# Moving half of the weight sums, and the second parts of weights, in a one-core decoder layer

## The chip, the cores and the metric

The kernel runs on one core of a Trainium2 chip. The core has five engines with instruction queues of their own: TensorE (PE; its weight loads are listed as PEld), VectorE (DVE), ScalarE (ACT), GpSimd (POOL) and SyncE (SP), which here issues nearly all DMAs. The metric is device time in microseconds (us) of one execution; the time before is the median of three runs. The profile is of one further execution.

## What is computed

One layer of a decoder, for a prompt of 2048 tokens and a sample group of 8 sequences of 8 tokens, with the same weights, in float32:

```python
def rmsnorm(x, w):
    return x * rsqrt(mean(x * x) + 1e-6) * w

proj = rmsnorm(x, norm_mix_w) @ w_in               # 1024 -> 8 x 512
rq, rk, rv, rg, hq, hf, hi, hg = split(proj, 8)    # 4 heads of 128 each
# retention heads: rotary on rq, rk; scalar decay per head
# HGRN2 heads: f = lb + (1 - lb) * sigmoid(hf), k = 1 - f
# both: S_t = diag(g_t) S_{t-1} + k_t^T v_t ;  o_t = q_t S_t   (chunkwise)
o = concat(head_rmsnorm(o_r) * silu(rg), head_rmsnorm(o_h) * silu(hg))
x = x + o @ w_out
x = x + square(relu(rmsnorm(x, norm_ffn_w) @ w_up)) @ w_down   # 1024 -> 4096 -> 1024
y = rmsnorm(x, final_norm_w)
```

The states S after the last token are outputs too.

## The kernel before, in words

The 2112 tokens are worked in three groups (`GROUPS`): 64 sample tokens with 512 of the prompt (576 columns), then twice 768 of the prompt. Each group goes through mixing (`mix`: per head the projections, then the recurrence in chunks of 128), the output projection, and the feed-forward. Activations stand with features on the 128 partitions and tokens along the row, in tiles of 768 columns ("slab", 46 of them, and 6 of a second kind, "ld").

Weights come as 128 x 1024 float32 blocks (512 KB). To multiply at nearly full float32 precision, each is split into two parts that TensorE's faster fp32r format can hold: `hi`, a rounded copy made by ScalarE (L269), and `lo` = raw - hi (L284), called the second part here, made by VectorE or GpSimd. Each product is hi x hi + hi x lo + lo x hi, three matmuls. `weight(i)` keeps two blocks ahead of the one in use; `hi` and `lo` have three buffers each, raw blocks of the first group two.

`plan_stream` lists the weights in order of use. For the first group, stream positions 0 to 39 are the input and output projections and 40 to 103 the 64 blocks of the feed-forward (`ffn_first`: up projections of one eighth of the 4096 features, `up_first`, then the down projections of the eighth before, `down_first`). The parts of positions 4 to 39 are written to DRAM once and read back ("p" entries) for groups two and three; only their first four blocks ("w" entries, positions 104 to 107 and 253 to 256) are split again.

Groups two and three compute their feed-forward with a seven-product scheme for 2 x 2 block products in place of eight (`PRODUCTS`, `OCTET`). It needs sums of weight blocks: S1 = A21 + A22, S3 = A11 - A21, S2 = S1 - A11, S4 = A12 - S2. `plan_sums` makes them: for each of 15 sets (7 of the up projection, 8 of the down projection), four loads, four VectorE additions of 128 x 1024 (L1273, tile `raw`), and four stores (L1278) to DRAM, from which the later groups load them as "s" entries.

The order of the work: the program puts instructions out in an order of its own and a scheduler orders them further within each engine; some are pinned with `keep_in_program_order` (the sums, their loads and stores among them). Each engine then works strictly in its order. In `proj`, every three-matmul product of a block calls `tick()`, which counts `n_ticks` and puts out whatever is due: work in `agenda` (through `at` and `later`) and the steps of `plan_sums` in `side`. So a tick is a place between matmuls, not a time. A block of weights has 8 sub-blocks with three products each: 24 ticks. The mixing of a later group has 4 heads with 192 ticks each, 768 in all; the first group's output projection and feed-forward have 192 + 1536 = 1728 ticks. Before, the 15 sets begin 90 ticks after the first mixing, one every 100 ticks, and within a set loads are at ticks 0, 12 and 24, additions at 40, 50, 60 and 70, stores at 60, 70, 80 and 90.

Other lines that matter: L1215 and L1151 are VectorE additions that empty a PSUM pair after a projection (`pj` has two pairs); L1202 and L1203 square the up projection's result on VectorE and cut it on GpSimd; L526 and L509 prepare the next group's input (`norm_in`); L1030 updates the state S, which L1017 multiplies (in a later group's head in 6 steps, one per chunk, 7 ticks apart); L348 and L482 cut tiles into two parts; L253 loads kept parts, L233 raw blocks.

The masks of the recurrence are 16 matrices of 128 x 128 zeros and ones, used as bytes (`msk`). `constants` gives them as float32; `masks` fetches them in four loads of 256 KB and GpSimd casts each to bytes (L451).

Of the kernel before, what the change touches and what calls it, by code (L numbers as in the profile page):

```python
# [15 lines left out]
P = 128  # L16
# [16 lines left out]
NLV = len(LEVELS) + 2  # L33
# [8 lines left out]
W_UP0 = W_OUT0 + N_OUT  # L42
W_DN0 = W_UP0 + N_UP
NQ = FF // (4 * P)
NO = NQ // 2

W_UQ0 = W_DN0 + N_DN
W_DQ0 = W_UQ0 + N_UP
# [50 lines left out]
def constants():  # L99
    c = np.zeros((P, NCONST), np.float64)  # L100
    c[:, C_ID:C_ID + P] = np.eye(P)
    s = np.arange(P)[:, None]
    t = np.arange(P)[None, :]
    sc = DK ** -0.5
    same = (s // SLEN == t // SLEN) & (s < NS) & (t < NS)
    for h, g in enumerate(GAM):
        dec = np.where(s <= t, g ** np.maximum(t - s, 0), 0.0) * sc
        c[:, C_RM + h * P:C_RM + (h + 1) * P] = dec
        c[:, C_RS + h * P:C_RS + (h + 1) * P] = np.where(same, dec, 0.0)
        c[:, C_GQ + h * P:C_GQ + (h + 1) * P] = g ** (t + 1.0)  # L110
        c[:, C_GS + h * NS:C_GS + (h + 1) * NS] = g ** (np.arange(NS) % SLEN + 1.0)
        c[:, C_KS + h] = sc * g ** (P - 1.0 - s[:, 0])
        c[:, C_KSS + h] = np.where(s[:, 0] < NS, sc * g ** (SLEN - 1.0 - s[:, 0] % SLEN), 0.0)
    c[:, C_SM:C_SM + NSEQ] = (s // SLEN == np.arange(NSEQ)[None, :])
    m = np.zeros((P, 2 * NLV, P), np.float32)
    for i, w in enumerate(LEVELS + (1,)):
        lv = (s // (2 * w) == t // (2 * w)) & (s % (2 * w) < w) & (t % (2 * w) >= w)
        m[:, i] = lv
        m[:, NLV + i] = lv & (s < NS) & (t < NS) & (w < SLEN)

    i = LEVELS.index(2)
    m[:, 0], m[:, NLV] = m[:, i] * (s % 2), m[:, NLV + i] * (s % 2)
    m[:, NLV - 1] = s == t
    m[:, 2 * NLV - 1] = (s == t) & (s < NS)
    half = DK // 2
    inv = np.power(10000.0, (-np.arange(half, dtype=np.float32) / np.float32(half)).astype(np.float64)).astype(np.float32)
    pos = np.concatenate([np.tile(PAST + np.arange(SLEN), NSEQ), np.arange(SEQ)]).astype(np.float32)
    ang = (inv[:, None] * pos[None, :]).astype(np.float64)
    cs = np.zeros((P, 2, NT), np.float32)
    cs[:half, 0] = cs[half:, 0] = np.cos(ang)  # L130
    cs[:half, 1] = -np.sin(ang)
    cs[half:, 1] = np.sin(ang)
    return c.astype(np.float32), m.reshape(P, -1), cs.reshape(P, -1)

# [63 lines left out]
class Kernel:  # L200
# [43 lines left out]
    def weight(self, i):  # L244
        n = len(self.stream)
        while self.w_next < min(i + 1 + self.ahead, n):
            j = self.w_next
            e = self.stream[j]
            if e[0] == "p":

                self.wts[j] = tuple(self.wp.tile([P, WT], F32R, tag=tag, name=tag) for tag in ("hi", "lo"))
                for part, kept in zip(self.wts[j], self.kept[e[1]]):
                    self.nc.sync.dma_start(part.bitcast(F32), kept)  # L253
                self.w_next += 1
                self.w_load = max(self.w_load, j + 1)
                continue
            while self.w_load <= j or j >= self.n_first and self.w_load <= j + 2 and self.w_load < n:
                if self.stream[self.w_load][0] == "p":
                    break
                k, later = self.w_load, self.w_load >= self.n_first  # L260
                raw = self.raws[k] = self.wp.tile([P, WT], F32, tag="sum" if later and k % 3 else "raw", name="raw",
                                                  bufs=4 if later and k % 3 else 2)
                e = self.stream[k]
                self.fetch(raw, self.sums[e[1]] if e[0] == "s" else self.I["w"][e[1]])
                self.w_load += 1
            raw = self.raws.pop(j)
            hi = self.wp.tile([P, WT], F32R, tag="hi", name="hi")
            lo = self.wp.tile([P, WT], F32R, tag="lo", name="lo")
            self.nc.scalar.copy(hi, raw)  # L269
            self.wts[j] = (hi, lo)  # L270
            self.second[j] = raw
            pool = self.stream[j][2] if len(self.stream[j]) > 2 else j % 4 and 3 < j
            if pool or j < 4:
                self.second_part(j, self.nc.gpsimd if pool else self.nc.vector)
            else:
                self.later(4, self.second_part, j, self.nc.vector)
            self.w_next += 1
        self.second_part(i, self.nc.vector)
        return self.wts[i]
# [87 lines left out]
    def build(self):  # L367
        nc, tc, I = self.nc, self.tc, self.I
        with ExitStack() as ctx:
# [19 lines left out]
            msk = cp.tile([P, 2 * NLV, P], U8, name="msk")  # L389
# [13 lines left out]
            for ns, p0, n in GROUPS:  # L403
# [4 lines left out]
                first = nch // 2  # L408
# [17 lines left out]
            nc.gpsimd.memset(self.ATs, 0.0)  # L426
            self.lower_bounds(cp)

            for i, g in enumerate(gs):
                nxt = gs[i + 1] if i + 1 < len(gs) else None  # L430
                if i == 0:
                    self.mix(g)
                    self.plan_sums(90, 100)
                    self.out_proj_first(g)
                    self.ffn_first(g, nxt)
                    continue
                if i == 1:
                    self.finish_first(gs[0])
                else:
                    self.finish(gs[i - 1])  # L440
                self.mix(g)
                self.out_proj(g)
                self.ffn(g, nxt)
            nc.sync.dma_start(self.O["ret_p"].rearrange("h d v -> d h v"), self.S[:, :H])
            nc.sync.dma_start(self.O["hg_p"].rearrange("h d v -> d h v"), self.S[:, H:])

    def masks(self):
        for i in range(0, 2 * NLV, 4):
            t = self.load()
            self.fetch(t[:, :4 * P], self.I["msk"][:, i * P:(i + 4) * P])  # L450
            self.nc.gpsimd.tensor_copy(self.msk[:, i:i + 4], t[:, :4 * P].rearrange("p (m t) -> p m t", t=P))  # L451

    def lower_bounds(self, cp):
        nc = self.nc
# [803 lines left out]
        self.later(4 * KB + 10, factor)  # L1258


    def plan_sums(self, first, every):
        nc, w = self.nc, self.I["w"]
        sets = [(("u", t), W_UQ0 + 4 * t) for t in range(1, NQ)]
        sets += [(("d", o, v), W_DQ0 + 4 * (2 * o + v)) for o in range(NO) for v in range(2)]
        self.side = deque()

        def load(x, i, *names):
            for name in names:
                x[name] = self.wp.tile([P, WT], F32, tag="sum", name="raw", bufs=4)
                self.tc.keep_in_program_order(nc.sync.dma_start(x[name], w[i + A_PLACE[name]]))  # L1270

        def make(x, name, a, op, b, into):
            self.tc.keep_in_program_order(nc.vector.tensor_tensor(out=x[into], in0=x[a], in1=x[b], op=op))  # L1273
            x[name] = x[into]

        def keep(x, key, name):
            s = self.sums[key + (name,)] = self.dp.tile([P, WT], F32, name="s" + "".join(map(str, key)) + name)
            self.tc.keep_in_program_order(nc.sync.dma_start(s, x[name]))  # L1278

        for j, (key, i) in enumerate(sets):  # L1280
            x, t = {}, self.n_ticks + first + every * j
            steps = [(0, load, x, i, "A21", "A22"), (12, load, x, i, "A11"), (24, load, x, i, "A12"),
                     (40, make, x, "S1", "A21", ALU.add, "A22", "A22"),
                     (50, make, x, "S3", "A11", ALU.subtract, "A21", "A21"),
                     (60, make, x, "S2", "S1", ALU.subtract, "A11", "A11"),
                     (70, make, x, "S4", "A12", ALU.subtract, "S2", "A12")]
            steps += [(d, keep, x, key, name) for d, name in ((60, "S1"), (70, "S3"), (80, "S2"), (90, "S4"))]
            for d, fn, *a in sorted(steps, key=lambda z: z[0]):
                self.side.append((t + d, lambda fn=fn, a=a: fn(*a)))
        self.side = deque(sorted(self.side, key=lambda z: z[0]))  # L1290
# [461 lines left out]
```

## Time and profile before

| | us |
|---|---|
| median of 3 runs | 2607.36 (2606.47 to 2609.86) |
| the profiled execution | 2605.96 |
| its span, first to last instruction | 2604.1 |
| TensorE busy | 2562.1 (98%) |
| VectorE busy | 1660.8 (64%) |
| ScalarE busy | 1161.2 (45%) |
| GpSimd busy | 932.4 (36%) |
| DMA | 441.32 MB, mean 169 GB/s |

How to read it: the times of the profile count from the first instruction. The first group's mixing ends near 300 us, its feed-forward near 796 us, the second group near 1690 us. Busy shares are means over stages with different limits, so the views of a stretch (windows, waits of one engine, timeline) say more than the page's totals. In the windows view each engine has its busy time and number of instructions, then the granted clock of TensorE, the share of the DMA engines' time, and GB/s. In a row of waits stand the engine and line that waited, the one that it waited for, total us, number, and longest. In a row of the timeline stand start, length, engine, line, operation, tiles, shape and count, and in brackets the idle time before it and what ended that. A group row has the count, busy time and mean duration in ns.

### The profile page before, as it was taken

Reading aid. Unit: us, or ns where it says so; the run is one execution under the profiler, and the core shown is the slowest. Engines: PE = TensorE matmul, PEld = TensorE weight load, DVE = VectorE, ACT = ScalarE, POOL = GpSimd, SP = SyncE. Lnnn points to the kernel's source line nnn. Section 1 sums busy time; section 2 is a strip of 40 time slices with the busy share of each in tenths; the row PEclk is TensorE's granted clock in tenths of the full one; section 3 lists DMA queues with packets and bytes.
Section 4 is the critical chain, followed back from the end, with each engine's and each line's share of the span. In section 5 each row is a group of like instructions: output and inputs, shape, how many; then the busy total and the mean of one; then the engine's idle time right before and its main releaser. Section 6 shows DMA issues by size and latency. Waiting matters only on the chain.

```text
span 2604.1 us, 41673 instructions
## 1 busy us (share of the span) xinstructions
PE 2562.1 (98%) x16999; PEld 2532.6 (97%) x16999; DVE 1660.8 (64%) x2072; ACT 1161.2 (45%) x1581; POOL 932.4 (36%) x538
## 2 busy tenths in 40 slices
PE   8999999999999999999999999999999999999997
PEld 8999999999999999999999999999999999999997
DVE  6666777554566455565554898775555555559876
ACT  6555442222244444444533544444444355345433
POOL 6555547444435133220222332341333012222322
PEclk9999999999999999999999999999999999999999
DMA  7566676666663322232555745442223326565542
GB/s 255 190 214 200 220 280 250 226 229 247 235 226 117 114 98 98 94 110 82 172 185 179 280 173 190 158 146 98 98 98 110 118 78 190 171 215 205 180 169 81
DMA packets 146689, 441.32 MB, mean 169 GB/s; under 512 B 14785, under 2 KB 36289, under 8 KB 146497
## 3 DMA queue, kind: packets, MB, share of 16 engines
q1 hardware_dynamic: 146352, 438.63, 49.1%
q8 instruction: 134, 2.20, 0.3%
q14 instruction: 59, 0.48, 0.1%
q10 hardware_dynamic: 144, 0.02, 0.0%
HBM read 330.85 MB, written 107.74 MB: 168 GB/s over the span
## 4 chain that ended last, share of the span: by engine, by line
PE 81%; DVE 4%; POOL 2%; issue 2%; ACT 1%; DMA 0%; DVEq 0%; POOLq 0%; ACTq 0%
PE pj L340 34%; PE pd L1123 16%; PE pu L1123 16%; PE pjv L705 5%; PE mm L1123 2%; PE mm L834 1%; PE po L1015 1%; PE mm L1023 1%; PE po L1017 1%; POOL lo L284 1%; DVE slab L509 1%; PE mm L891 1%; PE mm L488 1%; POOL slab L1178 1%; PE mm L487 1%
## 5 line engine op out<-in xcount | busy, mean ns | idle before, releaser
L340 PE MATMUL pj<-slab,hi 128*128 128x288 f32 (+1 forms) x5120 | 1016.2, 316 | 15.9 <-DVE slab L1215 7.2
L284 POOL TENSOR_TENSOR lo<-raw,hi 128x1024 fp32r<-128x1024 f32 x173 | 461.4, 2667 | 1079.4 <-ACT hi L269 993.8
L340 PEld LDWEIGHTS pj<-slab,hi 128*128 128x128 f32 x5120 | 810.9, 189 | 21.7 <-DVE slab L1215 8.1
L269 ACT CAST hi<-raw 128x1024 fp32r<-128x1024 f32 x330 | 347.0, 1051 | 746.9 <-PE pj L340 308.1
L340 PE MATMUL pj<-slab,lo 128*128 128x288 f32 (+1 forms) x2560 | 598.9, 315 | 1.4 <-POOL lo L284 1.2
L1123 PE MATMUL pd<-slab,hi 128*128 128x384 f32 x1792 | 456.9, 335 | 5.8 <-DVE slab L1568 2.1
L340 PEld LDWEIGHTS pj<-slab,lo 128*128 128x128 f32 x2560 | 429.2, 189 | 2.5 <-POOL lo L284 1.5
L1123 PE MATMUL pu<-slab,hi 128*128 128x384 f32 x1600 | 396.2, 334 | 0.0
L1123 PEld LDWEIGHTS pd<-slab,hi 128*128 128x128 f32 x1792 | 324.5, 188 | 7.1 <-DVE slab L1568 2.4
L284 DVE TENSOR_TENSOR lo<-raw,hi 128x1024 fp32r<-128x1024 f32 x157 | 208.3, 1327 | 146.2 <-ACT hi L269 142.9
L1123 PE MATMUL pd<-slab,lo 128*128 128x384 f32 x896 | 300.3, 335 | 0.9 <-POOL lo L284 0.9
L1123 PEld LDWEIGHTS pu<-slab,hi 128*128 128x128 f32 x1600 | 288.1, 188 | 0.0
L1123 PE MATMUL pu<-slab,lo 128*128 128x384 f32 x800 | 256.9, 334 | 0.0
L705 PE MATMUL pjv<-hi,slab 128*128 128x256 f32 x1088 | 208.5, 285 | 0.0
L1324 DVE TENSOR_TENSOR slab<-slab 128x768 fp32r<-128x768 f32 x144 | 162.0, 1140 | 33.4 <-ACT slab L1320 20.9
L705 PEld LDWEIGHTS pjv<-hi,slab 128*128 128x128 f32 x1088 | 173.4, 191 | 1.4
L1123 PEld LDWEIGHTS pd<-slab,lo 128*128 128x128 f32 x896 | 168.7, 188 | 1.5 <-POOL lo L284 1.5
L1320 ACT CAST slab<-slab 128x768 fp32r<-128x768 f32 x144 | 117.9, 833 | 105.4 <-DVE slab L1331 82.9
L705 PE MATMUL pjv<-lo,slab 128*128 128x256 f32 x544 | 153.8, 283 | 0.0
L1123 PEld LDWEIGHTS pu<-slab,lo 128*128 128x128 f32 x800 | 149.3, 188 | 0.0
L1538 DVE TENSOR_TENSOR slab<-pd,slab 128x768 f32<-128x768 f32 x110 | 104.2, 950 | 36.9 <-PE pd L1123 36.8
L1273 DVE TENSOR_TENSOR raw<-raw 128x1024 f32<-128x1024 f32 x60 | 104.8, 1746 | 0.6
(198 smaller groups left out, 3325.2 us busy)
## 6 DMA issues: line engine op xcount, KB each, us to landing
raw<-w SPq DMA_DIRECT2D x270, 512.0 KB, 4.4
u<-ld SPq DMA_DIRECT2D x64, 384.0 KB, 4.6
slab<-u SPq DMA_DIRECT2D x64, 384.0 KB, 5.7
ld<-x SPq DMA_DIRECT2D x32, 384.0 KB, 4.6
y<-slab SPq DMA_DIRECT2D x12, 384.0 KB, 2.7
raw<-su1S SPq DMA_DIRECT2D x8, 512.0 KB, 3.4
raw<-su2S SPq DMA_DIRECT2D x8, 512.0 KB, 4.0
raw<-su3S SPq DMA_DIRECT2D x8, 512.0 KB, 4.0
```

Of the source, the lines that this page charges most:

```text
L269: self.nc.scalar.copy(hi, raw)
L284: eng.tensor_tensor(out=lo, in0=self.second.pop(j), in1=hi.bitcast(F32), op=ALU.subtract)
L340: self.nc.tensor.matmul(pj[:, i, :T2], w, a[:, c0:c1], start=j == 0 and q == 0, stop=j == n - 1 and q == 2)
L487: self.nc.tensor.matmul(ps, self.ones_r, hi, start=True, stop=False)
L488: self.nc.tensor.matmul(ps, self.ones_r, lo, start=False, stop=True)
L509: (eng or nc.gpsimd).tensor_tensor(out=acc[:, :T], in0=acc[:, :T], in1=t[:, :T], op=ALU.add)
L705: nc.tensor.matmul(pj[:, i * 256:(i + 1) * 256], a[:, s:s + C], ww, start=kb == 0 and q == 0, stop=kb == KB - 1 and q == 2)
L1123: self.nc.tensor.matmul(*a, **k)
L1273: self.tc.keep_in_program_order(nc.vector.tensor_tensor(out=x[into], in0=x[a], in1=x[b], op=op))
L1320: self.nc.scalar.copy(hi[:, :g.T], B[name][:, :g.T])
L1324: self.nc.vector.tensor_tensor(out=lo[:, :g.T], in0=B[name][:, :g.T], in1=hi.bitcast(F32)[:, :g.T], op=ALU.subtract)
L1538: nc.vector.tensor_tensor(out=r, in0=ps, in1=r, op=ALU.add)
```

## The change

- `second_part` for weights: GpSimd made those at stream positions above 3 that are not a multiple of 4 (entries with a rule of their own aside). Now this holds for positions below 40 only. The other blocks of the first group's feed-forward, and the first four of groups two and three, get their second part from VectorE, put out four ticks after ScalarE's copy.
- `plan_sums` takes the sets, the first tick and the distance as arguments. The 7 up-projection sets stay in the first group, from tick 90 with one every 200. The 8 down-projection sets go beside the second group's mixing, from tick 100 with one every 84; what is left in `side` at its end is put out before the output projection.
- The masks are given as bytes and fetched in one load of 256 KB into their place, without a cast.

```diff
-    return c.astype(np.float32), m.reshape(P, -1), cs.reshape(P, -1)
+    return c.astype(np.float32), m.astype(np.uint8).reshape(P, -1), cs.reshape(P, -1)
...
-            pool = self.stream[j][2] if len(self.stream[j]) > 2 else j % 4 and 3 < j
+            pool = self.stream[j][2] if len(self.stream[j]) > 2 else j % 4 and 3 < j < W_UP0
             if pool or j < 4:
                 self.second_part(j, self.nc.gpsimd if pool else self.nc.vector)
             else:
...
+            sums = [(("u", t), W_UQ0 + 4 * t) for t in range(1, NQ)]
+            sums += [(("d", o, v), W_DQ0 + 4 * (2 * o + v)) for o in range(NO) for v in range(2)]
             for i, g in enumerate(gs):
                 nxt = gs[i + 1] if i + 1 < len(gs) else None
                 if i == 0:
                     self.mix(g)
-                    self.plan_sums(90, 100)
+                    self.plan_sums(sums[:NQ - 1], 90, 200)
                     self.out_proj_first(g)
                     self.ffn_first(g, nxt)
                     continue
                 if i == 1:
                     self.finish_first(gs[0])
+                    self.plan_sums(sums[NQ - 1:], 100, 84)
                 else:
                     self.finish(gs[i - 1])
                 self.mix(g)
+                while self.side:
+                    self.side.popleft()[1]()
                 self.out_proj(g)
                 self.ffn(g, nxt)
...
     def masks(self):
-        for i in range(0, 2 * NLV, 4):
-            t = self.load()
-            self.fetch(t[:, :4 * P], self.I["msk"][:, i * P:(i + 4) * P])
-            self.nc.gpsimd.tensor_copy(self.msk[:, i:i + 4], t[:, :4 * P].rearrange("p (m t) -> p m t", t=P))
+        self.fetch(self.msk.rearrange("p m t -> p (m t)"), self.I["msk"])
...
-    def plan_sums(self, first, every):
+    def plan_sums(self, sets, first, every):
         nc, w = self.nc, self.I["w"]
-        sets = [(("u", t), W_UQ0 + 4 * t) for t in range(1, NQ)]
-        sets += [(("d", o, v), W_DQ0 + 4 * (2 * o + v)) for o in range(NO) for v in range(2)]
         self.side = deque()
```

## The prediction

> **What bounds the kernel now.** I read the stretches of the program first (the view of windows), then TensorE's waits in each, and last the timeline around the longest waits.
>
> ```profile
> 0.00:300.00 300.00, 289.75 (x2243) 278.67 (x2244) 200.58 (x350) 176.38 (x283) 174.39 (x153) 1.00 0.64 212
> ...
> 400.00:738.00 338.00, 335.37 (x2507) 334.32 (x2508) 185.48 (x147) 90.78 (x110) 170.75 (x77) 1.00 0.66 235
> 738.00:796.00 58.00, 52.02 (x368) 50.98 (x367) 44.58 (x45) 26.20 (x35) 19.11 (x9) 0.97 0.54 188
> 796.00:1176.00 380.00, 380.00 (x2634) 375.53 (x2633) 213.19 (x356) 168.50 (x254) 121.65 (x86) 1.00 0.30 108
> ```
>
> The stretches are the first group's mixing, its feed-forward without and with its end, and the second group's mixing with its output projection; the columns are length, then busy time of PE, PEld, DVE, ACT, POOL, then clock, DMA share and GB/s. TensorE bounds the kernel: nothing that the change does can take a matmul away, so all it can win is TensorE's idle time. From 400 to 796 that is 2.63 + 5.98 = 8.6 us; in the second mixing it is zero. The first group's feed-forward therefore has everything to give, the second mixing has only something to lose.
>
> Who ended it (TensorE's waits, 300 to 823 us, so with the output projection ahead of the feed-forward; the same view from 823 to 1176 us is empty), three places in the timeline, and two windows of 3 us:
>
> ```profile
> PE pj L340 <- DVE slab L1215: 7.2, 5, 2.8
> PE pj L340 <- DVE slab L1151: 2.4, 2, 1.6
> PE pj L340 <- POOL lo L284: 1.2, 1, 1.2
> ...
> PE mm L488 <- DVE slab L482: 0.8, 1, 0.8
> ...
> 745.03 0.53 PE L340 MATMUL pj<-slab,hi 128*128 128x288 f32 x2 [2.82 <-DVE slab L1215]
> 766.49 0.79 PE L340 MATMUL pj<-slab,hi 128*128 128x288 f32 x4 [2.01 <-DVE slab L1215]
> 793.49 0.62 PE L340 MATMUL pj<-slab,hi 128*128 128x384 f32 x2 [1.13 <-DVE slab L1215]
> ...
> 768.00:771.00 3.00, 3.00 (x14) 3.00 (x13) 0.04 (x1) 0.00 (x0) 0.00 (x0) 0.50 0.37 150
> 772.00:775.00 3.00, 3.00 (x24) 3.00 (x24) 0.58 (x2) 0.06 (x1) 2.39 (x1) 1.00 0.00 0
> ```
>
> L1215 is the addition that empties the PSUM pair after a down projection; when VectorE is behind, both pairs are full and TensorE stops. 5.96 of its 7.2 us lie at the end of the feed-forward, and right behind the second stop the clock stands at 0.50: 14 matmuls in 3 us instead of 24, so 10 × 0.125 = 1.3 us lost there; I count 1.5 for the whole slow piece. In all 11.6 + 1.5 = 13.1 us are on the table.
>
> **Why VectorE is late there.** Rows of VectorE, then of GpSimd, from 738 to 766 us:
>
> ```profile
> 738.31 1.79 DVE L1273 TENSOR_TENSOR raw<-raw 128x1024 f32<-128x1024 f32 x1
> 740.02 3.15 DVE L526 SCALAR_TENSOR_TENSOR slab<-ld,vec,slab 128x768 fp32r<-128x768 f32 x1
> 743.10 1.21 DVE L1273 TENSOR_TENSOR raw<-raw 128x1024 f32<-128x1024 f32 x1
> 744.23 0.74 DVE L1215 TENSOR_TENSOR slab<-pj,slab 128x576 f32<-128x576 f32 x1
> 744.90 1.00 DVE L526 SCALAR_TENSOR_TENSOR slab<-ld,vec,slab 128x768 fp32r<-128x768 f32 x1
> 756.81 2.50 DVE L509 TENSOR_TENSOR slab<-slab 128x768 f32<-128x768 f32 x1
> 760.83 0.94 DVE L509 TENSOR_TENSOR slab<-slab 128x768 f32<-128x768 f32 x1
> 762.63 3.13 DVE L509 TENSOR_TENSOR slab<-slab 128x768 f32<-128x768 f32 x1
> ...
> 739.91 2.44 POOL L284 TENSOR_TENSOR lo<-raw,hi 128x1024 fp32r<-128x1024 f32 x1 [0.90 <-ACT hi L269]
> 755.83 2.67 POOL L284 TENSOR_TENSOR lo<-raw,hi 128x1024 fp32r<-128x1024 f32 x1 [13.46 <-ACT hi L269]
> 762.23 2.72 POOL L284 TENSOR_TENSOR lo<-raw,hi 128x1024 fp32r<-128x1024 f32 x1 [3.73 <-ACT hi L269]
> ```
>
> Two things hold VectorE up: two weight sums (L1273, 1.79 + 1.21 = 3.0 us), and three of its own operations that last 3.15, 2.50 and 3.13 us instead of 1.00, 0.94 and 0.94: each overlaps a weight's second part (L284) on GpSimd. That is 2.15 + 1.56 + 2.19 = 5.9 us. The Trainium skill ("SBUF — State Buffer", section "Who interferes with whom") says that a VectorE instruction with two SBUF inputs and a GpSimd instruction that reads SBUF exclude each other, the later one waiting to the other's end. The three rows agree.
>
> **The change, part by part.** Durations of L284 on GpSimd and on VectorE from 400 to 823 us as minimum/median/maximum, the page's group of L1273 (mean 1746 ns), and its row of weight loads:
>
> ```profile
> L284 POOL TENSOR_TENSOR lo<-raw,hi x47: 2382/2398/3350, 399.5 to 802.9; 128x1024 fp32r<-128x1024 f32 x47
> L284 DVE TENSOR_TENSOR lo<-raw,hi x15: 1214/1225/2448, 409.9 to 778.7; 128x1024 fp32r<-128x1024 f32 x15
> ...
> L1273 DVE TENSOR_TENSOR raw<-raw 128x1024 f32<-128x1024 f32 x60 | 104.8, 1746 | 0.6
> ...
> raw<-w SPq DMA_DIRECT2D x270, 512.0 KB, 4.4
> ```
>
> (1) Second parts. Stream positions 40 to 103 are the first group's 64 feed-forward weights; 48 second parts move from GpSimd (48 × 2.40 = 115 us off) to VectorE (48 × 1.23 = 59 us on). (2) Sums. 8 of the 15 sets, 32 additions, leave: 32 × 1.21 (the row at 743.10) = 39 us off VectorE alone, 56 at the mean. The other 7 sets come every 200 ticks instead of 100, so the last ends at tick 1380 instead of 1580 and is clear of the end. VectorE's own work in this stretch is thus about even; what falls is the exclusion by GpSimd.
>
> At the end of the feed-forward (738 to 766): off 3.0 + 5.9 = 8.9, on three second parts, 3 × 1.23 = 3.7: 5.2 us less in a stretch that now makes TensorE stop for 2.82 + 2.01 = 4.8. The first stop sits right behind the two sums and the 3.15 row, so all 2.8 go. For the second the margin is only 0.4 us, so I count 1.6 of 2.0, and 1.5 for the clock piece, which followed that stop. At 793 one more second part comes to VectorE; 0.4 of 1.1. The GpSimd wait goes whole: 1.2. The three small L1215 stops (7.2 − 5.96) go: 1.2. L482 and L1151: the first set, at its old tick, still stands before L1151; 0.8 of 3.2. Together 2.8 + 1.6 + 1.5 + 0.4 + 1.2 + 1.2 + 0.8 = 9.5 us won. Ends: 13.1 (all) and 4 (the first stop and the GpSimd wait alone).
>
> The new VectorE work is queued four ticks behind ScalarE's copy. If it waits for that copy, an emptying behind it waits too; a weight takes 24 ticks here, and the copy comes two weights ahead, so the data is never late itself:
>
> ```profile
> 726.03 1.05 ACT L269 CAST hi<-raw 128x1024 fp32r<-128x1024 f32 x1 [4.08 <-PE pj L340]
> 732.43 1.05 ACT L269 CAST hi<-raw 128x1024 fp32r<-128x1024 f32 x1 [4.08 <-PE pj L340]
> ...
> SPq L233 <- POOL lo L284: 156.7, 33, 13.4
> ```
>
> A weight lasts 6.40 us, so copy (1.05) and second part (1.23) end some 2.3 us after a weight begins, while an emptying falls due only after half a weight, 3.2: nothing, as long as the raw weight has landed. SyncE's weight loads now wait 156.7 us for GpSimd's second parts (400 to 823 us); those waits shorten.
>
> (3) The second mixing receives the 32 additions, and on SyncE's queue 32 loads and 32 stores of 512 KB: 33.6 MB in 380 us, 88 GB/s on top of 108, below the 235 of the feed-forward, so no DMA cost. VectorE goes from 213 to between 252 and 269 of 380 us, 66 to 71%; the first mixing runs at 67% beside a busier GpSimd. The tightest chain there is the recurrent state, S:
>
> ```profile
> 886.72 0.29 DVE L1030 SCALAR_TENSOR_TENSOR S<-S,mm 128x128 f32<-128x128 f32 x1 [2.04 <-PE mm L1023]
> 886.93 0.34 DVE L1030 SCALAR_TENSOR_TENSOR S<-S,slab,mm 128x128 f32<-128x128 f32 x1
> 888.83 0.39 PE L1017 MATMUL po<-slab,S 128*128 128x128 f32 x2
> ```
>
> S is ready at 887.27 and read at 888.83: 1.56 us to spare. An addition of 1.22 fits even if it starts at the last moment; one that GpSimd stretches to 2.4 (the longest VectorE row of L284 above, 2448 ns) does not, and costs 0.85. GpSimd is busy for 32% of this stretch, so some 10 of the 32 meet it; 8.5 us if all 10 stand ahead of S, nothing if VectorE's gaps of 2.04 us take them. The code updates S in 6 steps of 7 ticks out of a head's 192; 10 × 42/192 × 0.85 is 1.9, and I take 2.0.
>
> (4) Masks: four loads and four casts become one load.
>
> ```profile
> 25.70 3.15 POOL L451 CAST msk<-ld 128x512 uint8<-128x512 f32 x4 [2.75 <-DMA ld<-msk]
> 28.81 2.80 POOL L566 TENSOR_TENSOR ld<-ld,slab 128x576 f32<-128x576 f32 x2
> ```
>
> The rotary products right behind them can start at most 3.1 us earlier; no wait of TensorE follows. Zero either way, hidden by projections. (5) The first four weights of groups two and three also fall under the new rule: three second parts each, 3.7 us more on VectorE, at 795 and near 1690. Between 0 and 3.7 us; nearest is the row from 796 to 1176, where TensorE has no idle time at all, and I take 0.1.
>
> Sum: −9.5 + 2.0 + 0.1 = −7.4 us. The profiled execution took 2605.96 us (span 2604.1); 2598.6 of it remain. It lies 1.4 us below the median of 2607.36, so I predict 2600.0.
>
> **The rivals.** First, VectorE stays late (no measurable change): the 59 us of second parts, each waiting for ScalarE, fill what the sums leave; only the low end of 4 us is won, less 2 in the mixing: about 2605. For it: the narrow 0.4 us margin at 766. Against it: fewer long VectorE rows once GpSimd is still.
>
> Second, slower: sums late in the second mixing. SyncE's queue there (its waits, 823 to 1176 us), and two like places of successive heads in the chain of waits:
>
> ```profile
> SPq L253 <- PE pj L340: 248.1, 24, 12.6
> SPq L253 <- PE pjv L705: 70.8, 8, 17.4
> ...
> 852.25 1.95 PE pj L340 x10
> 940.39 1.95 PE pj L340 x10
> ```
>
> SyncE stands for 319 of 353 us before a kept weight whose buffer TensorE still reads. A set's loads are behind that. A head of 192 ticks lasts 88.1 us, 0.459 us a tick; the first addition comes 40 ticks or 18.4 us after its loads, of which landing takes 4.4: 14.0 us to spare. A wait of 12.6 fits, one of 17.4 is 3.4 too long: VectorE stands, and TensorE loses 3.4 − 1.56 = 1.8. If all 8 sets lost that on each of their first two additions it would be 29 us; from 15 us on, 9.5 plus the noise, the kernel is slower: about 2613 and more. Against it: a wait begins when the load heads the queue, so a load seldom meets a whole one.
>
> Third, all waits go and the mixing costs nothing: 2607.4 − 13.1 = 2594. For it: the rows stretched by GpSimd. Against it: the 0.4 us margin. The Trainium skill's rule on the shared port (the same section) would put every meeting in the mixing at its full length: then the 8.5 us above would be due, and the sum would be 2606.5.
>
> **Chances.** What the measurement can tell from no change is about 0.2%, 5.2 us: 2602.1 to 2612.6. Forecast (2600, own range 2596 to 2602) 0.45; all waits go 0.12; VectorE stays late, or meetings eat the gain (2602 to 2611) 0.27; slower 0.16. Hence faster 0.57, same 0.27, slower 0.16. The range 2593 to 2612 leaves out little but the slower case.
>
> **What would show it.** Right: no wait of TensorE on L1215 above 1 us before 796; GpSimd's L284 gone between 366 and 796; clock 1.00 there; VectorE near 250 to 270 us in the second mixing, TensorE idle 2 us or less. Wrong: TensorE waits on L1030, L348 or L482 in the second mixing; L1273 with idle time before it, ended by a load; L1215 late behind an L284 that waits for ScalarE.

## The result, and the profile after

| | before | after |
|---|---|---|
| median, executions on the same chip | 2607.28 us | 2593.80 us (four, 2591.08 to 2599.97) |
| ratio, with its 95% interval | | 0.995 [0.993, 0.9969] |
| the profiled execution | 2605.96 us | 2599.97 us |
| its span | 2604.1 us | 2598.2 us |

The change makes the kernel faster: 13.5 us by the medians, but only 6.0 us by the two profiled executions. The forecast was 7.4 us. The median of 2593.80 us lies below the forecast's own range of 2596 to 2602 us and just inside the wide one of 2593 to 2612. So there are two questions: whether the 6.0 us are made of the predicted parts, and what separates the profiled execution from the median.

The lines of the code have moved a little: L1215, L1151, L488 and L482 of before are L1217, L1153, L490 and L484 of after; L284, L340, L348 and L1273 are the same. The view of windows, of after, in the stretches of the prediction (length, busy time of PE, PEld, DVE, ACT, POOL, clock, DMA share, GB/s):

```profile
300.00:400.00 100.00, 97.43 (x724) 94.59 (x723) 66.63 (x94) 43.30 (x67) 35.06 (x21) 1.00 0.73 249
400.00:738.00 338.00, 337.75 (x2534) 337.51 (x2533) 171.56 (x164) 95.45 (x116) 64.02 (x36) 1.00 0.45 157
738.00:796.00 58.00, 57.98 (x409) 57.52 (x408) 40.39 (x49) 27.59 (x38) 5.56 (x3) 1.00 0.32 96
796.00:1176.00 380.00, 375.18 (x2597) 369.19 (x2596) 258.32 (x388) 165.29 (x250) 121.30 (x83) 1.00 0.56 200
```

The one row of before that the prediction does not show, from the same view:

```profile
300.00:400.00 100.00, 95.77 (x716) 92.70 (x714) 74.55 (x90) 42.93 (x67) 49.13 (x25) 1.00 0.81 274
```

The first two numbers of a row give TensorE's idle time:

| TensorE idle, us | before | after |
|---|---|---|
| 300 to 400 | 4.23 | 2.57 |
| 400 to 738 | 2.63 | 0.25 |
| 738 to 796 | 5.98 | 0.02 |
| 796 to 1176, second mixing | 0.00 | 4.82 |

In the first group 12.84 us became 2.84, and the clock from 738 to 796 rose from 0.97 to 1.00, which the prediction put at 1.5 us by estimate: 11.5 us won. The second mixing gives 4.8 back. That leaves 6.7, against 5.9 between the two spans.

What is left of TensorE's waits in after, first from 300 to 823 us, then from 800 to 1176 us (total us, number, longest):

```profile
PE pj L340 <- DVE slab L1153: 1.5, 2, 0.8
PE mm L490 <- DVE slab L348: 0.9, 1, 0.9
PE pj L340 <- DVE slab L1217: 0.2, 1, 0.2
```

```profile
PE pj L340 <- ACT slab L347: 1.4, 1, 1.4
PE mm L490 <- DVE slab L348: 1.4, 2, 1.0
PE mm L950 <- DVE AT L857: 1.2, 1, 1.2
PE mm L893 <- DVE slab L951: 0.6, 1, 0.6
PE mm L836 <- DVE AT L880: 0.2, 1, 0.2
```

The 7.2 us on L1215 are down to 0.2 and the wait for GpSimd's L284 is gone. The second mixing had no wait at all; now it has six stops, and none is on the state S, which the prediction had called the tightest chain there.

**Where the new stops come from.** In a head of a later group, masks are applied to the level products of the recurrence (L857 and L880, tile `AT`), and TensorE multiplies the result. VectorE in after, up to the longest stop on these products, one row of GpSimd, and the row of TensorE that stopped:

```profile
914.84 0.67 DVE L823 TENSOR_TENSOR slab<-slab 128x384 f32<-128x384 f32 x1 [1.61 <-ACT slab L817]
915.43 1.18 DVE L824 TENSOR_TENSOR slab<-slab 128x384 f32<-128x384 f32 x1
916.53 1.87 DVE L1273 TENSOR_TENSOR raw<-raw 128x1024 f32<-128x1024 f32 x1
918.33 1.18 DVE L868 TENSOR_TENSOR slab<-slab 128x384 f32<-128x384 f32 x1
919.43 1.24 DVE L823 TENSOR_TENSOR slab<-slab 128x384 f32<-128x384 f32 x1
...
922.87 1.04 DVE L857 COPY_PREDICATED AT<-msk,mm 128x384 f32<-128x384 uint8 x2
...
916.16 1.17 POOL L813 TENSOR_TENSOR slab<-slab 128x384 f32<-128x384 f32 x1
...
923.50 0.94 PE L950 MATMUL mm<-slab 128*128 128x128 f32 x6 [1.19 <-DVE AT L857]
```

Between two operations that ScalarE and TensorE wait for stands one addition, 1.87 us long because it overlaps GpSimd's work: it starts at 916.53 and GpSimd's row ends at 917.33. VectorE has no idle time there in which the delay could vanish. Experiment e4 below has no addition in this place, and its rows show the same sequence without it.

A plain addition can cost time too. At 1001 us one of 1.19 us stands two operations ahead of the cut (L348) that ended a stop of 0.99 us; the operation between them takes 1.58 us, against 0.92 in e4, where there is no addition and no stop:

```profile
1001.36 1.19 DVE L1273 TENSOR_TENSOR raw<-raw 128x1024 f32<-128x1024 f32 x1
1002.48 1.58 DVE L689 TENSOR_TENSOR slab<-slab 128x768 f32<-128x768 f32 x1
1003.98 1.59 DVE L348 TENSOR_TENSOR slab<-slab 128x768 fp32r<-128x768 f32 x1
...
1005.62 0.44 PE L490 MATMUL mm<-slab,ones_r 128*128 128x384 f32 x1 [0.99 <-DVE slab L348]
```

### The profile page after: what moved, and what is told of

It is laid out like the page before. It is cut to its first block, busy times and chain, and to the rows that moved or that the text cites. A ratio compares the mean times of both kernels' runs of the same rounds, so it can differ in the third digit from the quotient of the medians.

```text
span 2598.2 us, 41706 instructions
## 1 busy us (share of the span) xinstructions
PE 2561.3 (99%) x16999; PEld 2531.8 (97%) x16999; DVE 1676.9 (65%) x2126; ACT 1161.5 (45%) x1581; POOL 787.8 (30%) x480
## 4 chain that ended last, share of the span: by engine, by line
PE 81%; DVE 4%; issue 2%; POOL 1%; ACT 1%; DMA 1%; DVEq 0%; SPq 0%; POOLq 0%; ACTq 0%
PE pj L340 37%; PE pu L1125 16%; PE pd L1125 14%; PE pjv L707 5%; PE mm L1125 2%; PE mm L836 1%; PE po L1017 1%; PE mm L1025 1%; PE po L1019 1%; PE mm L490 1%; POOL lo L284 1%; DVE slab L348 1%; PE mm L893 1%; DVE lo L284 1%; PE mm L489 1%
## 5 line engine op out<-in xcount | busy, mean ns | idle before, releaser
L340 PE MATMUL pj<-slab,hi 128*128 128x288 f32 (+1 forms) x5120 | 1015.4, 316 | 9.5 <-ACT hi L269 6.2
L340 PEld LDWEIGHTS pj<-slab,hi 128*128 128x128 f32 x5120 | 810.7, 189 | 14.2 <-ACT hi L269 6.2
L269 ACT CAST hi<-raw 128x1024 fp32r<-128x1024 f32 x330 | 346.8, 1051 | 741.2 <-PE pj L340 354.3
L340 PE MATMUL pj<-slab,lo 128*128 128x288 f32 (+1 forms) x2560 | 598.4, 315 | 0.2 <-DVE lo L284 0.2
L284 POOL TENSOR_TENSOR lo<-raw,hi 128x1024 fp32r<-128x1024 f32 x119 | 322.1, 2706 | 898.0 <-ACT hi L269 826.8
L340 PEld LDWEIGHTS pj<-slab,lo 128*128 128x128 f32 x2560 | 428.9, 189 | 1.1 <-DVE lo L284 0.5
L284 DVE TENSOR_TENSOR lo<-raw,hi 128x1024 fp32r<-128x1024 f32 x211 | 273.4, 1296 | 224.9 <-ACT hi L269 220.9
L1205 POOL TENSOR_TENSOR slab<-slab 128x576 fp32r<-128x576 f32 x32 | 53.7, 1680 | 278.6 <-DVE slab L1204 278.6
```

The costliest lines, as they stand in the source:

```text
L284: eng.tensor_tensor(out=lo, in0=self.second.pop(j), in1=hi.bitcast(F32), op=ALU.subtract)
L340: self.nc.tensor.matmul(pj[:, i, :T2], w, a[:, c0:c1], start=j == 0 and q == 0, stop=j == n - 1 and q == 2)
L1205: nc.gpsimd.tensor_tensor(out=lo[:, :T], in0=r[:, :T], in1=hi.bitcast(F32)[:, :T], op=ALU.subtract)
```

## The experiments

Every kernel was executed at least five times. The ratio is to executions of the kernel before on the same chip; e1 to e4 share these, as do e5 to e8 and e9 to e11.

### What removes the stops of the first group

**e2**, the second parts alone, all 15 sets of sums left where they were:

```diff
-            pool = self.stream[j][2] if len(self.stream[j]) > 2 else j % 4 and 3 < j
+            pool = self.stream[j][2] if len(self.stream[j]) > 2 else j % 4 and 3 < j < W_UP0
```

> The kernel before with the second parts moved to VectorE and nothing else: all 15 sets of sums stay in the first group, 100 ticks apart. Theory A (VectorE was late above all because GpSimd's second parts shut it out): TensorE's idle time from 400 to 796 us falls from 8.6 to 3 us or less, the second mixing stays at zero, in all 2596 to 2600 us. Theory B (VectorE's own load was the cause, and the sums' leaving is what made room): 59 us more on VectorE with all the sums beside it make it later, idle time 8 us or more, 2606 us or slower.

Measured: 2595.53 us (2593.82 to 2596.68), ratio 0.9948 [0.9936, 0.996]. Its windows:

```profile
400.00:738.00 338.00, 337.75 (x2532) 337.29 (x2531) 200.29 (x189) 93.48 (x114) 64.03 (x37) 1.00 0.68 237
738.00:796.00 58.00, 57.98 (x414) 57.48 (x413) 43.66 (x53) 29.79 (x40) 5.56 (x3) 1.00 0.55 181
796.00:1176.00 380.00, 380.00 (x2633) 375.54 (x2632) 212.56 (x356) 164.79 (x249) 116.08 (x83) 1.00 0.31 108
```

VectorE is busier than before from 400 to 738 (200.29 us against 185.48), and still TensorE's idle time falls from 2.63 to 0.25 there and from 5.98 to 0.02 behind it. What fell is GpSimd's time (170.75 to 64.03), and with it the length of single VectorE operations: from 300 to 800 us the 32 squares of L1202 went from a mean of 1574 ns to 946 ns, the 60 additions of L1273 from 1746 ns to 1416 ns. So the stops came from VectorE's operations held up by GpSimd, not from VectorE's load. The Trainium skill ("SBUF — State Buffer", section "Who interferes with whom") says that a VectorE instruction with two SBUF inputs and a GpSimd instruction that reads SBUF shut each other out; that agrees with these windows.

**e3**, the sums alone moved, the second parts left on GpSimd:

```diff
-                    self.plan_sums(90, 100)
+                    self.plan_sums(sums[:NQ - 1], 90, 200)
...
+                    self.plan_sums(sums[NQ - 1:], 100, 84)
```

> The kernel before with the sums moved and nothing else: second parts stay on GpSimd. Theory A: at the end of the feed-forward only 3.0 of the 8.9 us go, TensorE's idle time from 400 to 796 us stays at 4 us or more, and the second mixing loses its 2 to 5 us: 2604 to 2609 us. Theory B: the idle time falls below 2 us and the total to 2600 us or less.

Measured: 2603.48 us (2601.06 to 2610.34), ratio 0.9981 [0.9973, 0.999]. Its windows:

```profile
400.00:738.00 338.00, 336.85 (x2563) 336.38 (x2562) 151.92 (x127) 97.37 (x118) 163.96 (x77) 1.00 0.48 159
738.00:796.00 58.00, 55.34 (x384) 54.15 (x384) 36.51 (x40) 24.80 (x33) 21.24 (x9) 1.00 0.31 93
796.00:1176.00 380.00, 375.09 (x2597) 369.13 (x2596) 257.49 (x389) 166.15 (x252) 121.86 (x84) 1.00 0.57 199
```

VectorE has lost 34 us from 400 to 738 and TensorE still stops for 2.66 us behind that, while the mixing loses 4.91. From 300 to 796 us its idle time is 7.24 us, against 12.84 before and 2.84 in after; from 400 us on it is 3.81 us, just under the 4 us or more that theory A named and far from the less than 2 us of theory B. By windows, then, either part helps the first group, the second parts more, and only the sums cost anything. The median lies 5.9 us below before, more than these stops give: by their times, 8 of the 11 executions (2601.06 to 2603.99 us) are of a quicker kind than the other three (2606.82 to 2610.34 us), which the section on the two paces takes up.

**e7**, the second parts and the byte masks, all sums in the first group:

```diff
+            pool = self.stream[j][2] if len(self.stream[j]) > 2 else j % 4 and 3 < j < W_UP0
...
+        self.fetch(self.msk.rearrange("p m t -> p (m t)"), self.I["msk"])
```

> The kernel before with the second parts on VectorE and the masks as bytes; all 15 sets stay in the first group, 100 ticks apart. The move of the down projection's sums is the only part undone. It costs the second mixing nothing (0 us idle there) and, if the masks are worth nothing, the first group loses nothing either: 2586 to 2596 us, about 6 us below the changed kernel in executions of the same kind.

Measured: 2593.83 us (2592.28 to 2596.18), ratio 0.9944 [0.993, 0.9957], against 0.9948 in e2. The masks' effect is not to be told from zero. Its second mixing has no stop, and against e1's slower kind (2602.3 of 2609.35, ratio 0.9973) it is 0.0029 lower, some 7.5 us where about 6 were expected.

### What the sums cost in the second mixing

**e4**, after without the eight down-projection sets:

```diff
-                    self.plan_sums(sums[NQ - 1:], 100, 84)
+                    for key, i0 in sums[NQ - 1:]:
+                        for name, a in (("S1", "A21"), ("S3", "A11"), ("S2", "A11"), ("S4", "A12")):
+                            self.sums[key + (name,)] = self.I["w"][i0 + A_PLACE[a]]
```

> The changed kernel without the sums of the down projection: the second and third groups take raw blocks in their place (so y of these groups is not the reference's), and no load, addition or store of sums stands beside the second mixing. If those additions are what stops TensorE there, its idle time from 796 to 1176 us falls from 4.8 us to 0.2 or less and the kernel takes 2588 to 2591 us; if the stops come from the four second parts moved to VectorE at the group's start or from the new order of instructions, 2 us or more remain and the time stays near 2593.

Measured: 2589.72 us (six executions: 2585.19, 2585.26, 2586.27, 2593.18, 2595.24, 2596.71), ratio 0.9929 [0.9914, 0.9943]. Its window of the second mixing, in which TensorE never stops:

```profile
796.00:1176.00 380.00, 380.00 (x2633) 375.54 (x2632) 212.52 (x356) 164.72 (x249) 115.78 (x83) 1.00 0.30 108
```

VectorE in the place of the stop shown above (two lines further down in this code: L857 is L859):

```profile
914.14 0.65 DVE L825 TENSOR_TENSOR slab<-slab 128x384 f32<-128x384 f32 x1 [1.62 <-ACT slab L819]
914.72 1.18 DVE L826 TENSOR_TENSOR slab<-slab 128x384 f32<-128x384 f32 x1
915.82 1.20 DVE L870 TENSOR_TENSOR slab<-slab 128x384 f32<-128x384 f32 x1
917.52 0.60 DVE L825 TENSOR_TENSOR slab<-slab 128x384 f32<-128x384 f32 x1 [0.50 <-ACT slab L819]
...
920.31 1.06 DVE L859 COPY_PREDICATED AT<-msk,mm 128x384 f32<-128x384 uint8 x2
```

From the first row to the masking it takes 920.31 − 914.14 = 6.17 us here and 922.87 − 914.84 = 8.03 us in after: 1.86 more, about the addition's own length. VectorE's only gap, 0.50 us, is used up in after, but the L823 behind it takes 1.24 us there instead of 0.60. TensorE lost 1.19 of the 1.86, so 0.67 us were to spare in this place.

**e5**, the same sets loaded and stored, but not added:

```diff
-            self.tc.keep_in_program_order(nc.vector.tensor_tensor(out=x[into], in0=x[a], in1=x[b], op=op))
+            if every != 84:
+                self.tc.keep_in_program_order(nc.vector.tensor_tensor(out=x[into], in0=x[a], in1=x[b], op=op))
```

> The changed kernel with the down projection's sums loaded and stored beside the second mixing, but not added (the stored blocks are the raw ones, so y of groups two and three is not the reference's). It parts VectorE's additions from SyncE's 64 transfers. Theory A (the additions fill the stretch of each head in which VectorE has no slack): TensorE's idle time from 796 to 1176 us is 0.2 us or less, as without the sums. Theory B (the transfers hold up SyncE's queue or the reads of kept weights): 2 us or more of the 4.9 us stay. As executions come in two kinds some 9.5 us apart, I expect times near 2586 or 2595 us under A, 2590 or 2599 us under B.

Measured: 2586.81 us (2583.66 to 2594.0), ratio 0.9918 [0.9904, 0.9931]. Its window of the second mixing:

```profile
796.00:1176.00 380.00, 380.00 (x2633) 375.54 (x2632) 206.98 (x349) 159.70 (x242) 113.94 (x82) 1.00 0.57 200
```

The DMA traffic is after's (200 GB/s) and TensorE never stops. The transfers are free; the additions are the cost.

**e6**, the sets set at chosen places of a head:

```diff
-                    self.plan_sums(sums[NQ - 1:], 100, 84)
+                    self.plan_sums(sums[NQ - 1:], 0, (44, 128, 212, 320, 404, 512, 596, 690))
```

> The changed kernel with the 8 sets of the second mixing begun at ticks 44, 128, 212, 320, 404, 512, 596 and 690 instead of every 84 from 100, so that the additions of a head fall between its stretches of level products (near 915, 1003 and 1091 us) instead of into them. Theory A (place decides): the stops at 915 to 933, at 997 to 1006 and at 1094 us go, 3.4 of 4.9 us, and at most 1.5 us stay. Theory B (VectorE's load or GpSimd's exclusion anywhere in the mixing decides): idle time stays at 4 us or more, at other places.

Measured: 2591.44 us (2589.93 to 2597.05), ratio 0.9936 [0.9924, 0.9949]. TensorE's waits from 800 to 1176 us:

```profile
PE pj L340 <- ACT slab L347: 1.6, 1, 1.6
PE mm L490 <- DVE slab L348: 1.0, 1, 1.0
PE mm L950 <- DVE AT L857: 0.8, 1, 0.8
```

After's stops between 923 and 1095 us are gone. Two new ones (817.5 and 826.9 us) belong to the set that this kernel begins earlier, at tick 44, and the one before 1135 stays with the last set, now before 1124. 3.4 us remain, more than expected: the first and the last set need other places.

**e9**, these two sets put back into the first group, nine there and six in the mixing at e6's places:

```diff
-                    self.plan_sums(sums[:NQ - 1], 90, 200)
+                    self.plan_sums(sums[:NQ + 1], 90, 160)
...
-                    self.plan_sums(sums[NQ - 1:], 100, 84)
+                    self.plan_sums(sums[NQ + 1:], 0, (128, 212, 320, 404, 512, 596))
```

> The changed kernel with nine sets in the first group, one every 160 ticks from 90, and six beside the second mixing, begun at ticks 128, 212, 320, 404, 512 and 596, between the level products of its heads. If place decides, the last stops of the second mixing go too (idle 0.3 us or less from 796 to 1176 us), and the kernel takes 2585 to 2588 us in executions with the quick pace of 288-column products and 2594 to 2597 us in the others. If VectorE's load there decides, 2 us or more stay.

Measured: 2594.02 us (2591.95 to 2596.92), ratio 0.9953 [0.9939, 0.9966]. Its window of the second mixing:

```profile
796.00:1176.00 380.00, 380.00 (x2633) 375.53 (x2632) 240.64 (x380) 164.73 (x249) 115.84 (x83) 1.00 0.52 180
```

24 additions, and not one stop. By their rows, 21 of them last 1.21 to 1.23 us and three 2.40 us; in after, 8 of the 32 last 1.85 to 2.86 us. So an addition that GpSimd stretches costs nothing in a place with room. e9 has eight additions fewer than after, but e6 has all 32, and none of its six sets from tick 128 to 596 makes TensorE stop. The place decides, not the engine's mean load. And yet the time is no better than after's. That is the second question.

### Two paces of TensorE

**e1** is after, unaltered.

> The changed kernel once more, unaltered. Its executions lie between 2591 and 2600 us, the profiled one at the top, and in that one TensorE stood still for 4.8 us in the second mixing. If that standstill differs from execution to execution, a second profile shows another idle time between 796 and 1176 us, between 0 and 5 us, and a total that differs by about as much; if it is fixed, the idle time is again 4.8 us and the spread lies elsewhere. I expect 2591 to 2596 us and 0 to 4 us of idle time there.

Measured: 2597.62 us, ratio 0.9957 [0.9943, 0.9971]; in six executions 2592.52, 2592.99, 2593.14 and 2602.11, 2602.30, 2602.64. The stops of the second mixing, which I had expected to vary, came again:

```profile
796.00:1176.00 380.00, 375.09 (x2595) 369.14 (x2595) 251.37 (x380) 160.04 (x242) 119.57 (x82) 1.00 0.56 198
```

They take 4.91 us here and 4.82 above, though the two profiled executions are 6.8 us apart. The stop near 427 us in the timeline of after, and in that of e1:

```profile
427.64 0.80 PE L340 MATMUL pj<-slab,hi 128*128 128x288 f32 x4 [0.25 <-DVE slab L1217]
```

```profile
427.49 0.80 PE L340 MATMUL pj<-slab,hi 128*128 128x288 f32 x4 [0.25 <-DVE slab L1217]
```

Two windows, before and behind that stop; first the profiled execution of after (2599.97 us), then that of e1 (2593.14 us):

```profile
368.00:427.00 59.00, 59.00 (x445) 59.00 (x444) 42.05 (x32) 25.93 (x37) 40.99 (x23) 1.00 0.43 151
429.00:759.00 330.00, 330.00 (x2477) 330.00 (x2476) 165.38 (x171) 96.56 (x117) 39.43 (x24) 1.00 0.47 161
```

```profile
368.00:427.00 59.00, 59.00 (x445) 59.00 (x443) 42.13 (x32) 25.93 (x37) 41.13 (x23) 1.00 0.44 149
429.00:759.00 330.00, 330.00 (x2541) 330.00 (x2540) 168.23 (x175) 98.35 (x119) 39.35 (x24) 1.00 0.50 163
```

Within these windows TensorE never stops, and the granted clock is 1.00. Up to 427 us both start 445 products; behind it one starts 2477 and the other 2541: one product each 330/2477 = 133.2 ns or each 330/2541 = 129.9 ns. The 64 products are worth 64 × 129.9 = 8.3 us. That is most of the 9.3 us between the two kinds of execution (medians 2602.3 and 2593.0).

ScalarE shows the same, so the count of products is not at fault. It copies one weight (L269) for every 48 products; the copies are 6.40 us apart in after (first two rows) and 6.24 us in e1 (last two):

```profile
440.46 1.05 ACT L269 CAST hi<-raw 128x1024 fp32r<-128x1024 f32 x1 [5.35 <-PE pj L340]
446.86 1.05 ACT L269 CAST hi<-raw 128x1024 fp32r<-128x1024 f32 x1 [5.35 <-PE pj L340]
...
440.02 1.06 ACT L269 CAST hi<-raw 128x1024 fp32r<-128x1024 f32 x1 [5.19 <-PE pj L340]
446.26 1.05 ACT L269 CAST hi<-raw 128x1024 fp32r<-128x1024 f32 x1 [5.18 <-PE pj L340]
```

e3, with its second parts on GpSimd, has the quicker pace too, but only for a stretch: from a stop of 0.29 us at 429 us to one of 0.86 us at 630 us. Its windows before and behind the second stop:

```profile
431.00:629.00 198.00, 198.00 (x1525) 197.89 (x1523) 83.50 (x72) 53.06 (x65) 87.41 (x42) 1.00 0.49 167
640.00:735.00 95.00, 95.00 (x714) 95.00 (x714) 35.83 (x32) 30.32 (x38) 41.10 (x20) 1.00 0.45 148
```

That is 129.8 ns a product, then 133.1 ns. Over some 200 us the quicker pace is worth about 5 us, by estimate most of the 5.9 us that e3's median lies below before.

**e8** gives all 15 sets other places in the first group (from tick 190, every 92), with e7's other edits:

```diff
-                    self.plan_sums(90, 100)
+                    self.plan_sums(190, 92)
```

> As the run before, with the 15 sets begun at tick 190 instead of 90, one every 92 ticks, so that none stands beside the output projection. The stops behind L1151 from 357 to 366 us, 1.6 us in all, are behind the first set's additions if those are their cause; then they go and the kernel is 1 to 2 us faster than the run before. If they are VectorE's own backlog of L1154, they stay.

Measured: 2593.19 us, ratio 0.9935 [0.9922, 0.9948]; four executions from 2592.74 to 2594.65, one of 2585.68. The wait on L1151 fell from 1.5 to 0.2 us, but one of the kind of L1215, 1.2 us long, appeared at 433.6: nothing gained. The one execution 7 to 9 us below the others looks like the quicker pace; it has no profile.

**e10** is e7 with all sums loaded and stored but none added, **e11** e7 with all additions but, of the loads and stores, only the first set's loads:

```diff
-            self.tc.keep_in_program_order(nc.vector.tensor_tensor(out=x[into], in0=x[a], in1=x[b], op=op))
```

> As e7 (second parts on VectorE, masks as bytes, all 15 sets in the first group), with the loads and stores of the sums but no additions (raw blocks are stored, so y of groups two and three is not the reference's). Of the executions of kernels with all sets in the first group one of 15 was of the quick kind, of those with half of them 17 of 26. If the transfers beside the first feed-forward keep TensorE at its slow pace, nearly all executions stay near 2593 us; if VectorE's additions do, about two of three lie near 2585 us.

```diff
+                if name not in held:
+                    held[name] = self.wp.tile([P, WT], F32, tag="sum", name="raw", bufs=4)
+                    self.tc.keep_in_program_order(nc.sync.dma_start(held[name], w[i + A_PLACE[name]]))
+                x[name] = held[name]
...
-            self.tc.keep_in_program_order(nc.sync.dma_start(s, x[name]))
```

> As e7, with the 60 additions of the sums but only the first set's four loads and no stores (the additions work on the same four tiles again and again, and groups two and three take raw blocks, so their y is not the reference's). If the transfers keep TensorE at its slow pace, about two of three executions lie near 2585 us; if the additions do, nearly all stay near 2593 us.

Measured: e10 2592.18 us (2591.94 to 2593.12), ratio 0.9943 [0.9931, 0.9956]; e11 2593.60 us (2592.90 to 2596.38), ratio 0.9951 [0.9939, 0.9963]. The same window of e10, then of e11:

```profile
429.00:759.00 330.00, 330.00 (x2477) 330.00 (x2476) 136.75 (x148) 97.38 (x118) 34.34 (x24) 1.00 0.72 244
```

```profile
429.00:759.00 330.00, 330.00 (x2478) 329.97 (x2477) 195.67 (x197) 95.71 (x115) 39.36 (x24) 1.00 0.32 98
```

Both have the slower pace, one with 244 GB/s and little VectorE work, the other with 98 GB/s and much. So taking away either one does not bring the quicker pace. Whether each is enough to keep the slower one, or neither matters, these two runs do not show. In e10 there is no stop at 427 us, so nothing in its place at which the pace could have changed.

**e12** therefore keeps the first seven sets at after's ticks, adds two late ones, and takes e9's places in the mixing:

```diff
-                    self.plan_sums(sums[:NQ - 1], 90, 200)
+                    self.plan_sums(sums[:NQ + 1], 0, (90, 290, 490, 690, 890, 1090, 1290, 1390, 1480))
...
-                    self.plan_sums(sums[NQ - 1:], 100, 84)
+                    self.plan_sums(sums[NQ + 1:], 0, (128, 212, 320, 404, 512, 596))
```

> The nine and six sets of e9, but with the first group's first seven sets at the changed kernel's own distance of 200 ticks and the other two at ticks 1390 and 1480. It parts two readings of the quick pace. If the pace is drawn anew at the one stop near 427 us that the changed kernel has (and e9 has not), and held until something disturbs it, the stop is back, about two of three executions lie near 2586 us and the rest near 2595 us. If the pace depends on how many sets stand beside the first feed-forward, all stay near 2593 us as in e9. The second mixing should again be without idle time.

Measured: 2594.23 us (2593.47 to 2595.01), ratio 0.9953 [0.994, 0.9967]. The mixing has no stop again, and the stop at 427 us is back (0.25 us), but all five times are those of the slower pace. The profiles of e2, e7 and e11 have the same stop of 0.25 us and the slower pace behind it, so the stop alone does not bring the quicker one. By their times, 17 of the 26 executions of the kernels with after's first group (after, e1, e4, e5, e6) were of the quicker kind, and none of the five of e12, which does the same up to tick 1290. On the one chip that e1 to e4 share, 14 of the 23 executions with seven sets in the first group (e1, e3, e4) were of the quicker kind, and none of the 22 with fifteen (before, e2). There the quicker pace goes with the moved sums, not with the second parts. But e9 to e12 ran on two other chips, on which no execution was of the quicker kind, so for them the chip is not excluded. What chooses the pace stays open.

## Why the prediction was right, and where it was not

**At one pace the sum holds.** Before kept the slower pace (1195 products in 159.30 us busy from 440 to 600 us: 133.3 ns). Against it stands the slower kind of e1, on the same chip: 2602.3 − 2609.35 = −7.05 us; the sum said −7.4. The profiled pair, both at the slower pace, gives −6.0. The mechanism in the first group was right too: L1215 is waited for 0.2 us at most, GpSimd's L284 is gone from 352 to 796 us, and the clock is 1.00.

**But two terms were too small, and that they offset each other is luck.** The first group was put at 9.5 and gave 11.5 by windows (13.8 by time in e2, 2.3 of which no window places). The additions in the mixing were put at 2.0 and cost 4.8 by windows; by time e1's slower kind lies 6.8 above e2, and 1.9 of that no window places.

- The first stop (2.8), the GpSimd wait (1.2) and the small L1215 stops (1.2, of which 0.2 stays) went as predicted, but L482 and L1151 fell together from 3.2 to 1.5 (the wait on L482 is gone), 1.7 where 0.8 was counted. The stop at 766 (1.6 of 2.0) and that at 793 (0.4 of 1.1) went whole. The margin of 0.4 us was too narrow a reading. The emptying whose end released TensorE at 766 before (the ninth from the last) is the first row here, in after. It ends at 755.22, 2.3 us before TensorE has filled the next pair, for which VectorE waits:

```profile
754.47 0.75 DVE L1217 TENSOR_TENSOR slab<-pj,slab 128x576 f32<-128x576 f32 x1
...
757.53 0.76 DVE L1217 TENSOR_TENSOR slab<-pj,slab 128x576 f32<-128x576 f32 x1 [0.22 <-PE pj L340]
```

- The failed step is the pricing of the additions on S: 10 meetings × 42/192 × 0.85. It assumed that a plain addition fits anywhere, because S has 1.56 us to spare. No stop is on S; the level products had 0.67, so there, by estimate, a plain 1.21 would already be 0.5 too long. The number of meetings was nearly right (8 stretched additions for 10), but where an addition stands decides: three of 2.40 us cost nothing in e9, and a plain one of 1.19 us stands ahead of a stop in after. Two of the signs of "wrong" came: TensorE waits on L348 in the second mixing (1.4 us), and a sum waited for its load. The idle time there is 4.8 us, where at most 2 would have been right.
- The Trainium skill's rule on the shared port ("SBUF — State Buffer", section "Who interferes with whom"), with every meeting at its full length, would by the prediction's estimate have cost 8.5 us in the mixing; 4.8 were measured.
- The first four weights of group three and the masks: nothing. TensorE's busy time from 1690 to 2074 us is 383.96 us in both traces; for the masks see e7.

**The rivals.** VectorE staying late is refuted by e2. The sums waiting for their loads did occur, once:

```profile
841.95 1.32 DVE L1273 TENSOR_TENSOR raw<-raw 128x1024 f32<-128x1024 f32 x1 [3.14 <-DMA raw<-w]
```

The wait is near the 3.4 us that were worked out, and TensorE lost nothing by it. The third rival's time, 2594, is the median's, but not for its reason: the mixing is not free.

**The step that no part of the prediction had** is the pace. It held that all the change can win is TensorE's idle time; at the quicker pace time is won while TensorE never stops. The median of 2593.80 is 6.2 us under the forecast, and by their times three of its four executions were of the quicker kind. The 17 executions of before beside e1 are of one kind (2606.61 to 2612.12), and so are e2's five. After's first group thus has the quicker pace more often, but the cause is open, so this part of the gain is observed and not explained. e2, which moves no sums and has the slower pace, is 2.1 us below e1's median on the same chip.

## What to carry to other kernels

When one engine delays another's consumer, look at how long single operations last before counting its load: in e2 VectorE got more work and became punctual, because GpSimd no longer held it up. Price filler work at its plain length against the tightest chain in each place where it can land, and choose the places, as e9 did. Set the profiled execution against the others before explaining the last 0.3%: here it stood 6 us above their median, as much as the change was worth in the profile.

## What the hardware showed unexpectedly

The same stream of 288-column products, with no stop and a granted clock of 1.00, ran for 330 us at 133.2 ns or at 129.9 ns a product, in executions of one and the same kernel. Up to a stop of 0.25 us the two executions were alike; behind it each held its pace up to 759 us, and in a second kernel (e3) the pace went back from 129.8 to 133.1 ns at a stop of 0.86 us. The Trainium skill ("TensorE: Matmul & The Clock Gate", section "Wait — 56ns, not 53.3ns?") gives N ÷ 2.4 GHz plus about 2.5 ns from start to start, which would be an estimate of 122.5 ns for 288 columns; both measured paces lie above it.
